# RWKV time mixing: batch 9 is transposed by the DMA crossbar instead of TensorE

## The chip, the cores and the metric

The kernel runs on one core of a Trainium2 chip. The metric is the device time of one execution in microseconds (us), the median over several runs. A core has the engines TensorE (PE, matrix products; its weight loads are listed apart as PEld), VectorE (DVE), ScalarE (ACT), GpSimd (POOL) and SyncE (SP, which here only issues transfers), and 16 DMA engines that all transfers share. Each engine works through its own instructions in order and waits on semaphores.

## The reference

16 batches of 2048 tokens with 256 channels, in float32. Each token is mixed with the one before it, by a weight for each channel; two projections, a sigmoid, a product and an output projection follow (the key projection does not reach the output).

```python
x_prev[:, 1:, :] = x[:, :-1, :]          # zeros for the first token
xv = x * time_mix_v + x_prev * (1 - time_mix_v)
xr = x * time_mix_r + x_prev * (1 - time_mix_r)
v = xv @ value_weight                    # 256 x 256 each
r = xr @ receptance_weight
out = (1 / (1 + exp(-r)) * v) @ output_weight
```

## The kernel before

**Tiling.** A batch is cut into 4 units of 512 tokens, 64 units in all, numbered through; unit 36 is the first of batch 9. The main loop runs over the units, `g`. All products run in bf16 with channels on the partitions, so x, which lies in memory with tokens in rows, has to be transposed. There are two ways:

- Batches 0 to 9: a transfer issued by POOL casts x to bf16 into an on-chip tile (`x_bf`, 4 buffers, pool `xpool`). TensorE transposes it, 8 transposes of 128 x 128 a unit (`transposes`, line 272), and ScalarE copies the result from PSUM into the transposed tile (line 289). This is done `LOOK` = 6 units ahead of use. Batches 0 and 1 have transposed tiles of their own (`xt_first0`, `xt_first1`), used by no one else afterwards; the others share tiles by groups (`GROUPS`), two buffers in turn (`xt_both`, pool `xtpool`).
- Batches 10 to 15 (from `STAGED` on): the casting transfer writes to a DRAM buffer (`x_natural`, pool `dpool`), 16 rows of zeros stand ahead of each batch (`zero_rows`), and one instruction on SP's queue reads a whole group of three batches back through the transposing crossbar into an `xt_both` tile (`by_dma`, line 254). It is issued in unit 27 for batches 10 to 12 and in unit 39 for 13 to 15 (`T_AT`).

**A unit on the engines.** The mixing is written as a scaled x plus the x of the token before, the rest of the factors being folded into the weights: two scaled tiles (for r and v) in two halves of the channels each. VectorE scales one half (line 354), POOL another (line 364, `scale_pool`, one instruction for two units), ScalarE one half of the v part from unit `FREE` on (line 638); VectorE adds (line 376). TensorE projects into `psum_r` and `psum_v` (line 384), ScalarE takes the sigmoid (line 658), VectorE multiplies into `z_sb` (line 697), TensorE makes the output product `psum_o` (line 416), ScalarE copies it to an output tile of two units (line 471), and SP stores this (line 437). `psum_r`, `psum_v` and `psum_o` have one buffer each. From unit `LATE_O` on, a unit's output product is made two units later rather than one. Output tiles take turns in 7 buffers of their own and in the 4 `x_bf` buffers once these hold no x any more (`SPARE`).

**Order.** It is the order of the code (the schedule is written by hand). Tables name the places: `LOADS` the unit whose transposes are due when a load is issued, `STAGE_AT` the units at whose end POOL issues the loads of batches 13 to 15. Three explicit dependencies tie the transfers together. A crossbar instruction waits until the last load before it has landed whole:

```python
op = nc.sync.dma_start_transpose(out=xt_both[b], in_=x_both[b].rearrange("b s d -> (b s) d"))
tc.add_manual_dep(op.ins, after.ins.name, SYNC, reason="not beside a load")
```

The loads of batches 13 to 15 wait, on POOL, until the last crossbar instruction so far (`last_t`) has landed:

```python
tc.add_manual_dep(op.ins, last_t.ins.name, SYNC, reason="not beside transposes")
```

And stores of some units (`FIRST`) wait for the first half of the last load, others (`WAITING`) are issued behind the crossbar instruction.

Of the kernel before, what the change touches and what calls it, by code (L numbers as in the profile page):

```python
# [9 lines left out]
BF16 = mybir.dt.bfloat16  # L10
# [5 lines left out]
def kernel(  # L16
# [27 lines left out]
    B, S, D = x.shape  # L44
    P = 128
    KO = D // P
    J = S // P
    UJ = 4
    TU = UJ * P
    UB = J // UJ  # L50
# [2 lines left out]
    BYUNIT = 2  # L53
    LONG = 2
    H = UJ // 2
    STAGED = 10
    BYDMA = NU - STAGED * UB
    CROSS = NU - BYDMA - LOOK
    FREE = CROSS
    LATE_O = CROSS - 2  # L60
    T_AT = {27: 10, 39: 13}
    FIRST = {19: 27, 21: 27, 27: 39}
    WAITING = {23: 27, 25: 27, 29: 39, 31: 39, 33: 39, 35: 39}
    ZEROS_AT = 12
    SINGLE = NU - 6
    STAGED_PAIRS = range(STAGED, B - 1)
    STAGE_AT = {33: 13, 34: 14, 35: 15}
    GROUPS = [(2, 3), (4, 5, 6), (7, 8, 9), (10, 11, 12), (13, 14, 15)]
    HALVED = (12, 15)
    PAD = 16  # L70
    SPARE = 9 * UB // 2
    NX, NO = 4, 7
    START_T = [1, 3, 5, 6, 7, 9, 11, 12]
    AHEAD = 6
# [7 lines left out]
        (2, 0): (5,),  # L82
        (3, 0): (6,),
        (4, 0): (7,),
        (5, 0): (8, 10),
        (6, 0): (9,),
        (7, 0): (11,),
        (7, 1): (12,),
    }

    consts = ctx.enter_context(tc.tile_pool(name="consts", bufs=1))
    xpool = ctx.enter_context(tc.tile_pool(name="xpool", bufs=NX))
    dpool = ctx.enter_context(tc.tile_pool(name="dpool", bufs=2, space=bass.MemoryType.DRAM))
    xtpool = ctx.enter_context(tc.tile_pool(name="xtpool", bufs=2))
    mixpool = ctx.enter_context(tc.tile_pool(name="mixpool", bufs=3))
    zpool = ctx.enter_context(tc.tile_pool(name="zpool", bufs=3))
# [15 lines left out]
    loads = {}  # L112
    xt_both = {}
    xt = {}
# [18 lines left out]
    def new_staged(group):  # L133

        x_both[group[0]] = dpool.tile([len(group), PAD + S, D], BF16, name="x_natural")
        for k in range(len(group)):
            x_bf[group[0] + k] = x_both[group[0]][k, PAD:].rearrange("(p j) d -> p j d", p=P)
        return [(group[0], k) for k in range(len(group))]
# [8 lines left out]
    def load(b):  # L147
        if b < STAGED:
            x_bf[b] = xpool.tile([P, J, D], BF16, name="x_bf")
        if b < BYUNIT:  # L150
            for e in range(UB):
                nc.gpsimd.dma_start(  # L152
                    out=x_bf[b][:, e * UJ : (e + 1) * UJ, :], in_=unit_rows(x, b, e)[:, 0]
                )
            return
        if b in HALVED:
            return [
                nc.gpsimd.dma_start(out=x_bf[b][:, j : j + J // 2], in_=rows(b)[:, j : j + J // 2])
                for j in (0, J // 2)
            ]  # L160
        run = 8192 if b < LONG else 16384
        return nc.gpsimd.dma_start(out=x_bf[b], in_=rows(b), max_dma_last_dim=run)  # L162
# [47 lines left out]
    def new_xt(b):  # L210
        if b >= BYUNIT:
            for group in GROUPS:
                if b != group[0]:
                    continue
                if b >= STAGED:
                    t = xtpool.tile([P, KO, len(group) * (PAD + S)], BF16, name="xt_both")
                    for k in range(len(group)):
                        xt[b + k] = t[:, :, k * (PAD + S) + PAD - 1 : (k + 1) * (PAD + S)]
                    xt_both[b] = t
                    return  # L220
                xt_both[b] = xtpool.tile([P, J + 1, KO, len(group), P], BF16, name="xt_both")
                for k in range(len(group)):
                    xt[b + k] = xt_both[b][:, :, :, k]
                    nc.gpsimd.memset(xt[b + k][:, 0, :, 0:1], 0.0)
            return
        xt[b] = consts.tile([P, UB * (UJ + 1), KO, P], BF16, name=f"xt_first{b}")
        (nc.vector if b == 0 else nc.gpsimd).memset(xt[b][:, 0, :, 0:1], 0.0)

    new_xt(0)
    tms = consts.tile([P, 2, KO], FP32)  # L230
    c_sb = consts.tile([P, 2, KO], FP32)
# [19 lines left out]
    def by_dma(b, after):  # L251

        new_xt(b)
        op = nc.sync.dma_start_transpose(
            out=xt_both[b], in_=x_both[b].rearrange("b s d -> (b s) d")
        )
        tc.add_manual_dep(op.ins, after.ins.name, SYNC, reason="not beside a load")
        return op
# [55 lines left out]
    def slots(piece, off=0):  # L314

        b, _, lo, hi = piece
        j = lo // P + (lo // TU if b < BYUNIT else 0) + off
        return slice(j, j + (hi - lo) // P)
# [6 lines left out]
    def tokens(piece, off, ko=None):  # L325

        b, _, lo, hi = piece
        if b in STAGED_PAIRS:
# [3 lines left out]
            return cols if ko is None else cols[:, ko]  # L332
        if b < STAGED:
            cols = xt[b][:, slots(piece, off)]
# [71 lines left out]
    def out_matmuls(ps, z, b, jj, n, whole=False):  # L406
# [3 lines left out]
        else:  # L410
            cols = z[:, :, jj * P : (jj + n) * P]
            order = "p k (j c) -> p k j c" if b < STAGED else "p k (c j) -> p k j c"
            slot = cols.rearrange(order, j=n)
# [35 lines left out]
    def new_o(b, h):  # L449

        n = b * UB // 2 + h - SPARE
        spare = n >= 0 and n % (NO + NX) < NX
# [109 lines left out]

    pads = [p for group in GROUPS if group[0] >= STAGED for p in new_staged(group)]
    tnext = 1

    def advance(limit):
        nonlocal tnext
        while tnext <= min(limit, NU - 1):
            b, e = divmod(tnext, UB)
            for n in LOADS.get((b, e), ()):  # L570
                loads[n] = load(n)
            if tnext < NU - BYDMA:
                transposes(tnext)
            tnext += 1
# [47 lines left out]
    for u in range(2, NU):  # L622
# [3 lines left out]
        for m, (b, _, lo, hi) in enumerate(pieces(u)):  # L626
            w = first[u][m]
            group = (b, m, lo, hi + TU if paired else hi)
# [17 lines left out]
    for g in range(NU - 1):  # L646
        ps_r = ps_r_pool.tile([P, KO, TU], FP32, name="psum_r")
        if g == 0:
            project_unmixed(ps_r, 0)
            advance(1)  # L650
            project_unmixed(ps_r, 1)
            wrap_slots(pieces(1)[0])
            scale(pieces(1)[0])
            last = add(pieces(1)[0])
        else:
            project(ps_r, g, 0)
        s_sb = zpool.tile([P, KO, TU], BF16, name="s_sb")
        nc.scalar.activation(out=s_sb, in_=ps_r, func=ACT.Sigmoid)  # L658
        advance(START_T[g] if g < len(START_T) else g + LOOK)
        if g in T_AT:  # L660
            half, whole = loads[T_AT[g] + 2]
            for pair in firsts.pop(g):
                store(nc.sync, *pair, after=half)
            last_t = by_dma(T_AT[g], whole)
            for pair in kept.pop(g, []):
                store(nc.sync, *pair)
        if LATE_O < g < NU - 2:
            output(g - 2, z_prev2)
        for p in products.get(g + 1, []):
            if g >= FREE and p[0][1] == 1:  # L670
                scale_act(p[0], (0,))
        for p in [q for q, _ in products[g]] + pooled[g]:
            last_unit_of = p[3] // TU - 1
            need = last_unit_of if p[0] < BYUNIT else min(last_unit_of + 1, UB - 1)
            assert UB * p[0] + need < tnext, (g, p, tnext)
            if g > AHEAD or p not in pooled[g]:
                wrap_slots(p)
        if g == 1:
            load(2)
            scale_act(pieces(2)[1], (1,))  # L680
        for p, kos in products[g]:
            if not (g - 1 >= FREE and p[1] == 1):
                scale(p, kos)
        for p in sums[g]:
            last = add(p)
        for p in pooled[g]:
            if p[0] >= BYUNIT:
                wrap_slots(p)
        ps_v = ps_v_pool.tile([P, KO, TU], FP32, name="psum_v")
        project(ps_v, g, 1)  # L690
        if g == 0:
            scale_act(pieces(1)[1], (0,))
            advance(2)
        z_sb = zpool.tile([P, KO, TU], BF16, name="z_sb")
        n = TU // 2 if g == NU - 2 else TU
        for c in range(0, TU, n):
            nc.vector.tensor_tensor(  # L697
                out=z_sb[:, :, c : c + n],
                in0=s_sb[:, :, c : c + n],
                in1=ps_v[:, :, c : c + n],  # L700
                op=ALU.mult,
            )
        for p in pooled[g]:
            wrap_slots(p, after=last)
            scale_pool(p, last)
        if ZEROS_AT <= g < ZEROS_AT + len(pads):
            zero_rows(*pads[g - ZEROS_AT])
        if g in STAGE_AT:
            b = STAGE_AT[g]
            loads[b] = load(b)  # L710
            for op in loads[b] if b in HALVED else [loads[b]]:
                tc.add_manual_dep(op.ins, last_t.ins.name, SYNC, reason="not beside transposes")
        for p in held[g]:
            add(p)
        if z_prev is not None and not LATE_O <= g < NU - 3:
            output(g - 1, z_prev)
        z_prev2, z_prev = z_prev, z_sb
# [31 lines left out]
```

## Time and profile before

| | us |
|---|---|
| median of 3 runs | 199.1 (198.86 to 199.21) |
| the profiled execution, first to last instruction | 197.1 |
| TensorE busy | 191.5 |
| VectorE busy | 183.1 |
| ScalarE busy | 177.1 |
| POOL busy | 86.3 |
| crossbar instructions, issue to landing (median of 2) | 17.3 |

The profile gives the profiled execution as its span; no total of its own beside that is printed. A row of instructions in time has its start, its duration, the engine, the line and operation, the tile written and those read with their shapes, how many, and in brackets the idle time of the engine before it and what ended it. "SPq" is a transfer's issue on SP's queue: its duration is that of the issue, not of the transfer. A transfer's landing is given apart, in us from its issue.

### The profile page before, as it was taken

How to read it: one execution, taken by the hardware profiler on the slowest of the kernel's cores; microseconds unless marked ns; L12 is line 12 of the kernel's file. 1: busy time of each engine (PE TensorE's matmuls, PEld its weight loads, DVE VectorE, ACT ScalarE, POOL GpSimd, SP SyncE). 2: the span in 40 equal slices, each digit the busy share in tenths (PEclk: the TensorE clock that was granted, in tenths of full speed). 3: DMA queues.
4: the chain of work that ended last, by engine and by line, in shares of the span. 5: the costliest groups of instructions: out<-in, count | busy, mean ns of one | idle time of the engine just before them, and what ended most of it. 6: DMA issues, size and time to landing. Idle time of an engine off the chain costs nothing.

```text
span 197.1 us, 3735 instructions
## 1 busy us (share of the span) xinstructions
PE 191.5 (97%) x1358; PEld 123.0 (62%) x1364; DVE 183.1 (93%) x286; ACT 177.1 (90%) x197; POOL 86.3 (44%) x117
## 2 busy tenths in 40 slices
PE   8999999999999999999999999999999999999992
PEld 3556676666666666666666666666666666666660
DVE  0999999999999999999999999999999999999962
ACT  3699899999999999999999999999999999999982
POOL 2845542443665635624334266444433444444200
PEclk9999999999999999999999999999999999999998
DMA  5999999999999999999999999999999999999985
GB/s 185 238 176 224 218 254 262 247 259 262 296 413 283 283 296 332 283 238 198 376 209 290 335 346 186 212 218 241 290 290 419 419 421 419 416 416 421 382 327 221
DMA packets 35593, 58.13 MB, mean 295 GB/s; under 512 B 26004, under 2 KB 27128, under 8 KB 30840
## 3 DMA queue, kind: packets, MB, share of 16 engines
q1 hardware_dynamic: 31792, 41.34, 60.3%
q0 software_dynamic: 3632, 16.44, 41.6%
q8 instruction: 10, 0.16, 0.3%
q10 hardware_dynamic: 152, 0.13, 0.2%
q14 instruction: 7, 0.06, 0.1%
HBM read 34.34 MB, written 39.90 MB: 377 GB/s over the span
## 4 chain that ended last, share of the span: by engine, by line
PE 90%; DMA 6%; POOL 1%; issue 0%; SPq 0%; ACT 0%
PE psum_r L384 27%; PE psum_v L384 27%; PE psum_o L416 27%; PE ps_t L272 8%; DMA x_bf<-in_x_dram 4%; DMA w_f<-n_receptance_weight_dram 2%; PE ps_t L416 1%; POOL x_bf L192 1%; SPq L174 0%; POOL wo_bf L195 0%; PE psum_v L416 0%; POOL x_bf L152 0%; PE ps_t L384 0%; PE psum_r L416 0%; ACT x_bf L446 0%
## 5 line engine op out<-in xcount | busy, mean ns | idle before, releaser
L364 POOL TENSOR_SCALAR mix<-xt_both,c_sb 128x1024 bf16<-128x1024 bf16 (+1 forms) x55 | 61.1, 1110 | 85.5 <-DVE mix L376 82.3
L697 DVE TENSOR_TENSOR z_sb<-s_sb,psum_v 128x1024 bf16<-128x1024 bf16 (+1 forms) x64 | 76.8, 1201 | 2.3 <-PE psum_v L384 1.1
L376 DVE TENSOR_TENSOR mix<-mix,xt_both 128x1024 bf16<-128x1024 bf16 x112 | 76.8, 696 | 1.4
L384 PEld LDWEIGHTS <-w_bf 128*128 128x128 bf16 x512 | 48.5, 98 | 39.2 <-DVE mix L376 0.8
L658 ACT ACTIVATE s_sb<-psum_r 128x1024 bf16<-128x1024 f32 x63 | 65.2, 1034 | 6.2 <-PE psum_r L384 6.0
L384 PE MATMUL psum_v<-mix,w_bf 128*128 128x512 bf16 (+1 forms) x252 | 64.8, 378 | 0.4 <-DVE mix L376 0.2
L384 PE MATMUL psum_r<-mix,w_bf 128*128 128x512 bf16 x250 | 64.6, 379 | 0.2
L416 PE MATMUL psum_o<-wo_bf,z_sb 128*128 128x256 bf16 x486 | 63.2, 273 | 0.0
L416 PEld LDWEIGHTS <-z_sb 128*128 128x128 bf16 x512 | 52.0, 103 | 17.9 <-DVE z_sb L510 0.7
L471 ACT COPY o_sb<-psum_o 128x1024 f32<-128x1024 f32 x50 | 51.2, 1023 | 5.0 <-PE psum_o L416 4.8
L289 ACT COPY xt_both<-ps_t 128x1024 bf16<-128x1024 bf16 x32 | 32.9, 1039 | 0.0
L272 PEld LDWEIGHTS <-x_bf 128*128 128x128 bf16 x304 | 19.8, 98 | 8.4 <-DMA x_bf<-in_x_dram 0.4
L272 PE MATMUL ps_t<-ident,x_bf 128*128 128x128 bf16 x304 | 22.7, 219 | 0.2 <-DMA x_bf<-in_x_dram 0.2
L354 DVE TENSOR_SCALAR mix<-xt_both,c_sb 128x1024 bf16<-128x1024 bf16 (+1 forms) x47 | 21.3, 463 | 0.0
L638 ACT ACTIVATE mix<-xt_both,c_sb 128x1024 bf16<-128x1024 bf16 x14 | 16.3, 1163 | 0.0
L376 DVE TENSOR_TENSOR mix<-mix,xt_first 128x1024 bf16<-128x1024 bf16 x15 | 10.5, 708 | 0.1
L471 ACT COPY x_bf<-psum_o 128x1024 f32<-128x1024 f32 x10 | 10.2, 1015 | 0.0
L354 DVE TENSOR_SCALAR mix<-xt_first,c_sb 128x512 bf16<-128x512 bf16 x22 | 6.6, 350 | 0.3 <-ACT xt_first L282 0.2
L289 ACT COPY xt_first<-ps_t 128x1024 bf16<-128x1024 bf16 x6 | 6.0, 1022 | 0.0
L557 POOL COPY xt_first<-xt_first 128x254 bf16<-128x254 bf16 x5 | 2.0, 392 | 7.2 <-DVE mix L376 7.2
L162 POOL DMA_DIRECT2D x_bf<-in_x_dram x8 | 4.7, 584 | 0.0
L364 POOL TENSOR_SCALAR mix<-xt_first,c_sb 128x512 bf16<-128x512 bf16 x6 | 4.1, 685 | 1.3 <-DVE mix L376 0.8
(68 smaller groups left out, 52.3 us busy)
## 6 DMA issues: line engine op xcount, KB each, us to landing
out_dram<-o_sb SPq DMA_DIRECT2D x25, 1024.0 KB, 12.1
x_bf<-in_x_dram POOLq DMA_DIRECT2D x8, 1024.0 KB, 15.8
x_natural<-in_x_dram POOLq DMA_DIRECT2D x4, 1024.0 KB, 11.8
out_dram<-x_bf SPq DMA_DIRECT2D x4, 1024.0 KB, 14.4
x_natural<-in_x_dram POOLq DMA_DIRECT2D x4, 512.0 KB, 12.7
out_dram<-x_bf SPq DMA_DIRECT2D x4, 512.0 KB, 4.7
x_bf<-in_x_dram POOLq DMA_DIRECT2D x6, 256.0 KB, 7.0
o_sb<-in_x_dram SPq DMA_DIRECT2D x4, 256.0 KB, 3.9
```

Source lines behind the costliest of these rows:

```text
L162: return nc.gpsimd.dma_start(out=x_bf[b], in_=rows(b), max_dma_last_dim=run)
L272: nc.tensor.transpose(out=ps[:, jj], in_=src[:, jj, ko * P : (ko + 1) * P], identity=idn)
L289: nc.scalar.copy(out=xt[b][:, j0 : j0 + UJ], in_=ps)
L354: nc.vector.tensor_scalar(out=mixed(piece, ko), in0=tokens(piece, 0, ko), scalar1=c_sb[:, m, ko : ko + 1], scalar2=None, op0=ALU.mult,)
L364: op = nc.gpsimd.tensor_scalar(out=mixed(piece, 1), in0=tokens(piece, 0, 1), scalar1=c_sb[:, m, 1:2], scalar2=1.0, op0=ALU.mult, op1=ALU.mult,
L376: return nc.vector.tensor_tensor(out=mixed(piece), in0=mixed(piece), in1=tokens(piece, 1), op=ALU.add)
L384: nc.tensor.matmul(out=ps[:, mo, :], lhsT=w_bf[:, m, ko, mo * P : (mo + 1) * P], rhs=mixed((b, m, e * TU + lo, e * TU + hi), ko), start=(k ...
L416: nc.tensor.matmul(out=ps[:, j, :], lhsT=slot[:, ko, j], rhs=wo_bf[:, ko, :], start=(ko == 0), stop=(ko == KO - 1),)
L471: nc.scalar.copy(out=o[:, j0 : j0 + UJ, :], in_=ps)
L638: nc.scalar.activation(out=mixed(piece, ko), in_=tokens(piece, 0, ko), func=ACT.Copy, scale=c_sb[:, m, ko : ko + 1],)
L658: nc.scalar.activation(out=s_sb, in_=ps_r, func=ACT.Sigmoid)
L697: nc.vector.tensor_tensor(out=z_sb[:, :, c : c + n], in0=s_sb[:, :, c : c + n], in1=ps_v[:, :, c : c + n], op=ALU.mult,)
```

## The change

Batch 9 joins the staged batches: it is cast into DRAM, gets its rows of zeros, and is transposed by a crossbar instruction of its own, issued in unit 27 just ahead of the one for batches 10 to 12. Its transposed tile is put in the memory of `xt_first0`, batch 0's tile, which moves to a pool `firstpool` of one buffer. The loads of batches 9 and 10 change places. `last_t` is, as before, the instruction for batches 10 to 12. `BYDMA` grows by 4, so `CROSS`, `FREE` and `LATE_O`, which hang on it, come down by 4 (`FREE` from 34 to 30, `LATE_O` from 32 to 28). `x_bf` buffers pass to the outputs two tiles earlier (`SPARE`).

```diff
-    STAGED = 10
+    STAGED = 9
...
-    T_AT = {27: 10, 39: 13}
+    T_AT = {27: (9, 10), 39: (13,)}
...
-    GROUPS = [(2, 3), (4, 5, 6), (7, 8, 9), (10, 11, 12), (13, 14, 15)]
+    GROUPS = [(2, 3), (4, 5, 6), (7, 8), (9,), (10, 11, 12), (13, 14, 15)]
...
-    SPARE = 9 * UB // 2
+    SPARE = STAGED * UB // 2 - 2
...
-        (5, 0): (8, 10),
-        (6, 0): (9,),
+        (5, 0): (8, 9),
+        (6, 0): (10,),
...
-    dpool = ctx.enter_context(tc.tile_pool(name="dpool", bufs=2, space=bass.MemoryType.DRAM))
+    dpool = ctx.enter_context(tc.tile_pool(name="dpool", bufs=3, space=bass.MemoryType.DRAM))
+    firstpool = ctx.enter_context(tc.tile_pool(name="firstpool", bufs=1))
...
-                    t = xtpool.tile([P, KO, len(group) * (PAD + S)], BF16, name="xt_both")
+                    pool, name = (firstpool, "xt_first0") if len(group) == 1 else (xtpool, "xt_both")
+                    t = pool.tile([P, KO, len(group) * (PAD + S)], BF16, name=name)
...
-        xt[b] = consts.tile([P, UB * (UJ + 1), KO, P], BF16, name=f"xt_first{b}")
+        xt[b] = firstpool.tile([P, UB * (UJ + 1), KO, P], BF16, name=f"xt_first{b}")
...
-            half, whole = loads[T_AT[g] + 2]
+            half, whole = loads[T_AT[g][-1] + 2]
             for pair in firsts.pop(g):
                 store(nc.sync, *pair, after=half)
-            last_t = by_dma(T_AT[g], whole)
+            for b in T_AT[g]:
+                last_t = by_dma(b, whole)
             for pair in kept.pop(g, []):
                 store(nc.sync, *pair)
```

How it stands in the queues, in two places. First SP, around the crossbar instructions; brackets name the semaphores waited for (those of transfers begin with DMAHW or DMASW). Before, ahead of it the store of a `FIRST` pair, behind it the two stores of `WAITING`, the store of the pair of units 26 and 27, and the second crossbar instruction:

```order
L437 DMA out_dram<-o_sb 128x2048 [waits DMAHW2_49,Activation_49]
L254 DMA_TRANSPOSE xt_both<-x_natural 128x2x6192 [waits DMASW5_49,DMASW1_49,DMASW6_49,DMASW0_49,DMAHW3_49,DVE_49,Pool_49]
L437 DMA out_dram<-o_sb 128x2048 [waits DMAHW4_49,Activation_49]
L437 DMA out_dram<-o_sb 128x2048 [waits DMAHW5_49,Activation_49]
L437 DMA out_dram<-o_sb 128x2048 [waits DMAHW6_49,DMASW3_49,Activation_49]
L254 DMA_TRANSPOSE xt_both<-x_natural 128x2x6192 [waits DMASW2_49,DMASW1_49,DMASW4_49,DVE_49,DMAHW7_49,Activation_49,Pool_49]
```

And in the changed kernel:

```order
L439 DMA out_dram<-o_sb 128x2048 [waits DMAHW2_49,Activation_49]
L256 DMA_TRANSPOSE xt_first_1404<-x_natural 128x2x2064 [waits DMASW5_49,DMASW1_49,DMAHW3_49,DVE_49,PE_49]
L256 DMA_TRANSPOSE xt_both<-x_natural 128x2x6192 [waits DMASW6_49,DMASW5_49,DMASW7_49,DMASW2_49,DMAHW4_49,DVE_49,Pool_49]
L439 DMA out_dram<-o_sb 128x2048 [waits DMAHW5_49,Activation_49]
L439 DMA out_dram<-o_sb 128x2048 [waits DMAHW6_49,Activation_49]
L439 DMA out_dram<-o_sb 128x2048 [waits DMAHW7_49,DMASW4_49,Activation_49]
L256 DMA_TRANSPOSE xt_both<-x_natural 128x2x6192 [waits DMASW3_49,DMASW5_49,DMASW2_49,DMASW6_49,DVE_49,DMAHW0_49,Activation_49,Pool_49]
```

The instruction for batch 9 (2064 rows) has moved in ahead of that for batches 10 to 12 (6192 rows), between the same stores.

Second POOL, from unit 33 on, where the loads of batches 13, 14 and 15 (the last in two halves) stand between its scalings. Before, the first scaling of this piece reads batch 9 in `xt_both`, and the load of batch 13 waits for the first crossbar instruction (DMAHW3):

```order
L364 TENSOR_SCALAR mix_194<-xt_both_1190,c_sb_134 128x8x128 [waits DVE_49,Activation_49]
L162 DMA x_natural_137<-in_x_dram 128x4096 [waits DMAHW3_49,DMASW1_49]
L364 TENSOR_SCALAR mix_194<-xt_both_1190,c_sb_134 128x8x128 [waits DVE_49]
L162 DMA x_natural_137<-in_x_dram 128x4096 [waits DMASW2_49]
L364 TENSOR_SCALAR mix_195<-xt_both_1190,c_sb_134 128x8x128 [waits DVE_49,PE_49]
L158 DMA x_natural_137<-in_x_dram 128x2048 [waits DMASW3_49]
L158 DMA x_natural_137<-in_x_dram 128x2048 [waits DMASW4_49]
```

In the changed kernel:

```order
L366 TENSOR_SCALAR mix_198<-xt_first0_1404,c_sb_137 128x128x2x4 [waits DMAHW3_49,DVE_49,PE_49]
L163 DMA x_natural_141<-in_x_dram 128x4096 [waits DMAHW4_49,DMASW2_49]
L366 TENSOR_SCALAR mix_198<-xt_first0_1404,c_sb_137 128x128x2x4 [waits DVE_49]
L163 DMA x_natural_141<-in_x_dram 128x4096 [waits DMASW3_49]
L366 TENSOR_SCALAR mix_199<-xt_first0_1404,c_sb_137 128x128x2x4 [waits DVE_49,PE_49]
L159 DMA x_natural_141<-in_x_dram 128x2048 [waits DMASW4_49]
L159 DMA x_natural_141<-in_x_dram 128x2048 [waits DMASW5_49]
```

The loads keep their places among the scalings; the first scaling now waits for batch 9's crossbar instruction (DMAHW3) and the load of batch 13 for the one of batches 10 to 12 behind it (DMAHW4).

## The prediction

> **What bounds the kernel now.** I read the page first: its engine shares, its slices, its DMA queues.
>
> ```profile
> span 197.1 us, 3735 instructions
> PE 191.5 (97%) x1358; PEld 123.0 (62%) x1364; DVE 183.1 (93%) x286; ACT 177.1 (90%) x197; POOL 86.3 (44%) x117
> DMA  5999999999999999999999999999999999999985
> DMA packets 35593, 58.13 MB, mean 295 GB/s; under 512 B 26004, under 2 KB 27128, under 8 KB 30840
> ```
>
> TensorE is 97% busy, so its work looks like the price of the kernel. But the DMA row is full too, from the second slice to the last but two. The profiled execution took 197.1 us from first to last instruction; its own total is not on the page, and the median of the runs, 199.1, lies 2.0 us above the span. I add all differences to 199.1.
>
> Then stretches with different traffic, each row with TensorE, weight loads, VectorE, ScalarE and POOL busy time, the granted clock (1.00 everywhere here), the share of the 16 DMA engines and their rate:
>
> ```profile
> 102.50:110.00 7.50, 7.50 (x62) 4.94 (x61) 7.18 (x11) 7.09 (x9) 2.24 (x2) 1.00 1.28 289
> 120.00:130.00 10.00, 9.95 (x61) 5.90 (x61) 9.98 (x14) 9.18 (x11) 5.18 (x6) 1.00 1.03 211
> 155.00:180.00 25.00, 24.84 (x154) 16.14 (x156) 24.94 (x34) 22.95 (x25) 11.21 (x10) 1.00 1.01 418
> ```
>
> The first is the crossbar alone, the second casting loads alone (counted by the bytes written), the third stores alone. The share is a sum over packets that can overlap, so 1.28 means full, not more than full. In each kind of traffic the engines have nothing to spare: stores run at 418 GB/s, loads at 211, crossbar transposes at 289. The kernel therefore stands against two walls, TensorE and the transfers, and VectorE (9.98 of 10, 24.94 of 25) is hard behind TensorE.
>
> Last I read the queues in order of time, at the place the change moves. SP issues the stores and the transposes, POOL its third of the mixing and the casting loads:
>
> ```profile
> 92.85 1.82 SPq L437 DMA_DIRECT2D out_dram<-o_sb  x2
> 95.38 15.20 SPq L254 DMA_TRANSPOSE xt_both<-x_natural  x1
> 110.67 0.52 SPq L437 DMA_DIRECT2D out_dram<-o_sb  x1
> ...
> xt_both<-x_natural SPq DMA_TRANSPOSE x1, 18.8
> ...
> 113.48 1.12 POOL L364 TENSOR_SCALAR mix<-xt_both,c_sb 128x1024 bf16<-128x1024 bf16 x1 [2.33 <-DVE mix L376]
> 114.71 0.56 POOL L162 DMA_DIRECT2D x_natural<-in_x_dram  x1
> 116.23 1.11 POOL L364 TENSOR_SCALAR mix<-xt_both,c_sb 128x1024 bf16<-128x1024 bf16 x1 [0.96 <-DVE mix L376]
> 117.30 0.55 POOL L162 DMA_DIRECT2D x_natural<-in_x_dram  x1
> ```
>
> The crossbar instruction for batches 10 to 12 is issued at 95.38 and lands 18.8 us later, at 114.18. The POOL instruction at 114.71 is the load of batch 13, which waits for that landing by the kernel's own rule. POOL ended its scaling at 114.60, so the landing came 0.4 us before POOL could have issued the load anyway: the wait costs nothing today, and has almost no slack.
>
> **The change, part by part.**
>
> *Taken off TensorE:* 32 transposes, 8 in each of units 30 to 33.
>
> ```profile
> 110.77 0.61 PE L272 MATMUL ps_t<-ident,x_bf 128*128 128x128 bf16 x8
> 111.21 1.04 PE L416 MATMUL psum_o<-wo_bf,z_sb 128*128 128x256 bf16 x8
> ```
>
> The next group starts 0.44 us after the transposes: 4 x 0.44 = 1.8 us less for TensorE, all on its path since it never idles there. ScalarE loses 4 evacuations and gains 2 scalings, VectorE loses 2 scalings and a small copy; so VectorE can follow at the shorter pace, as it does from unit 34 on now. All this could give is -1.8.
>
> *Added to the transfers:* the batch is read and cast as before, into DRAM instead of on-chip memory (the same bytes; its price is the loads' rate, 211 GB/s in the row above). New is its passage through the crossbar: 2064 x 256 x 2 bytes = 1.06 MB at 289 GB/s = 3.65 us. The zero rows, 8 KB, I cost at nothing: they queue behind a load.
>
> *A second instruction.* Its own start-up has no row. The nearest is the second crossbar instruction of before:
>
> ```profile
> 136.50:137.50 1.00, 1.00 (x8) 0.55 (x6) 1.00 (x2) 1.00 (x2) 0.51 (x1) 1.00 0.40 36
> xt_both<-x_natural SPq DMA_TRANSPOSE x1, 15.7
> ```
>
> Issued at 133.86, it shows a hole near its beginning: 0.60 us of the 1.00 us are empty. Its 3.17 MB at 289 GB/s take 11.0 us, so of 15.7 us issue to landing 4.7 are not flow. The bounds for the second start are thus 0 (the issue of the next runs under the packets of the first) and 4.7 (nothing overlaps). A gain below 0 is excluded: the bytes of batches 10 to 12 are the same. I take 0.5, near the hole, because both stand in one queue and SP's issue of a crossbar instruction ends before its packets do. So X, the delay of the landing for batches 10 to 12, is 3.65 + 0.5 = 4.1 us, between 3.65 and 8.4. The start does not move: both crossbar instructions still wait for the last load of batch 12, and stand behind the same two stores. The landing is then at 114.2 + 4.1 = 118.3.
>
> The Trainium skill, page "Advanced Engine Details and Errata", section "X-Bar Transpose (TRN2)", says that transposing DMAs are as fast as ordinary ones. The rows here disagree, 289 GB/s against 418, and by its rule X would be 2.5 with no other term changed, which is a rival below.
>
> *What waits for that landing.* POOL now reaches the load of batch 13 earlier, at 114.60 - 1.8 = 112.8, and stands there until 118.3. Queued behind it is its next scaling (116.23 now), then the loads of 14 and 15. The scaling feeds VectorE:
>
> ```profile
> 117.19 1.30 DVE L376 TENSOR_TENSOR mix<-mix,xt_both 128x1024 bf16<-128x1024 bf16 x2
> 118.46 1.22 DVE L697 TENSOR_TENSOR z_sb<-s_sb,psum_v 128x1024 bf16<-128x1024 bf16 x1
> 119.60 0.71 DVE L376 TENSOR_TENSOR mix<-mix,xt_both 128x1024 bf16<-128x1024 bf16 x1
> ...
> 117.33 1.03 PE L384 MATMUL psum_v<-mix,w_bf 128*128 128x512 bf16 x4
> 119.93 0.81 PE L384 MATMUL psum_v<-mix,w_bf 128*128 128x512 bf16 x3
> ```
>
> The second of the two additions (about 117.84) takes the POOL scaling that ended at 117.34, 0.5 us before. Behind it on VectorE stands the product of unit 35 (118.46 to 119.68), and that must have emptied the one psum_v bank before TensorE's next value projection, 119.93: 0.25 us of slack. Now forward: landing 118.3, load issued by 118.95, scaling to 120.06, addition to 120.7, product to 121.9, projection at 121.95 instead of 119.93. That is +2.0 against before, and the 1.8 us are already spent in it: TensorE arrives at 118.15 and waits 3.8 us. In general the shift is X + 3.65 + 114.2 - 119.93 = X - 2.1. Nothing later gives it back, since VectorE has no idle time left in the stretches from 120 to 180 above.
>
> *The transfers to the end.* Everything behind the crossbar in the queues slides by X: loads 13 to 15, the second crossbar instruction, the held stores. Is batch 13 late next? Its transposed tile lands at 133.86 + 15.7 = 149.6 now, 153.7 then. The first reader:
>
> ```profile
> 155.00 1.12 POOL L364 TENSOR_SCALAR mix<-xt_both,c_sb 128x1024 bf16<-128x1024 bf16 x1 [1.30 <-PE psum_v L384]
> ```
>
> It will be at 157.0, so 3.3 us remain, no new wait. The stores drain at 418 GB/s and arrive at the end with a backlog that is X - 2.0 = 2.1 us deeper relative to the work. Before, the transfers have holes only here:
>
> ```profile
> 186.50:187.50 1.00, 1.00 (x8) 0.55 (x6) 1.00 (x2) 1.00 (x2) 0.00 (x0) 1.00 0.62 246
> 189.50:191.00 1.50, 1.50 (x12) 1.06 (x11) 0.57 (x1) 1.27 (x4) 0.00 (x0) 1.00 0.39 156
> 192.00:194.50 2.50, 1.35 (x9) 0.54 (x8) 1.18 (x3) 1.34 (x3) 0.00 (x0) 1.00 0.79 302
> ```
>
> 0.38 + 0.91 + 0.52 = 1.8 us. So the transfers by themselves end X - 1.8 = +2.3 later. The two walls give +2.0 and +2.3; they run side by side, so the larger counts. Sum: 199.1 + 2.3 = 201.4, and I say 201.5 for the small packets at the end.
>
> *At nothing:* the other layout of batch 9's tile. POOL's scaling takes 1.12 us at 113.48 (slot layout) and 1.12 us at 155.00 (crossbar layout). The memory of batch 0's tile was read out in units 0 to 3, long before unit 27. The on-chip buffers freed for outputs change no wait that I can find: each output half still has 11 buffers in turn.
>
> **Rivals.**
>
> 1. *A dearer second start.* If the second crossbar instruction shares nothing with the first, X = 8.4: TensorE +6.3, transfers +6.6, 205.7. For it: 4.7 us of the 15.7 are not flow. Against: the first instruction's 15.20 us of issue on SP end before its landing by 3.6, so the next one starts under it. With 1.5 us of start, X = 5.2 and 202.5.
>
> 2. *Faster: the landing is not late.* The one way to gain is that POOL does not stand at the load, so that TensorE keeps its 1.8 us: 197.3. This takes a crossbar instruction whose passage for batch 9 overlaps that of 10 to 12, with X under 0.25, and the transfers' 1.8 us of holes at the end taking the rest; the price of the passage decides, and the kernel gains from X below 1.8. For it: the crossbar's packets are small, and the 289 GB/s could be the rate of one instruction rather than of the engines. Against: the share of 1.28 there, and that one queue issues both.
>
> 3. *A crossbar pass at the copy rate.* 1.06 MB at the stores' 418 GB/s is X = 2.5: TensorE +0.4, transfers +0.7, so 199.8. The Trainium skill's sentence above is this rule; the row 102.50:110.00 speaks against it. With X between 1.4 and 2.2 the time stays within 0.4 us, which is 0.2% and about what a measurement of this kernel can tell from no change.
>
> **How the numbers follow.** My own case, X from 3.65 to 5.2, 200.9 to 202.6: 0.72. Rival 1 beyond 5.2, to 205.7: 0.09. Rival 3: 0.08, a quarter of it within 0.2%. Rival 2: 0.08 faster. The remaining 0.03 is a shift within 0.2% by some cover I overlooked. Faster 0.08, same 0.05, slower 0.87. The predicted time is my case's, 201.5. The range leaves out rival 2, the no-change cases and the far end of rival 1: 199.8 (rival 3) to 203.6 (X = 6.3).
>
> **What the profile after would show.** Right: two crossbar issues in a row on SP from about 95.4, the second landing near 118; POOL idle some 5 us ahead of the load of batch 13, released by that transfer; an idle stretch of about 4 us on VectorE and then on TensorE near 118 to 122, the only one; 272 transposes on TensorE, not 304; the DMA share without holes to the end. Wrong: if the landing is before 115, the crossbar price is wrong; if it is late but TensorE has no gap, the chain POOL, VectorE, TensorE is; if the gap is there and the end is later by much more than it, the transfers are the wall alone. If the first crossbar issue comes well before 95.4, the whole sum moves with it.

## The result, and the profile after

The changed kernel takes 206.55 us (median of 4 runs, 204.94 to 206.97) against 199.16 us (198.86 to 199.56) for the kernel before beside it: ratio 1.0343, interval 1.0307 to 1.0379. Run again it took 205.25 us (204.27 to 205.43, 5 runs; ratio 1.0289, 1.0266 to 1.0311). The forecast was 201.5, from 199.8 to 203.6: the direction was right, the size was not. Ratios leave out runs that took over 1.5% longer than the fastest of their kernel, so a median over all runs can lie above what its ratio says.

From the page of the changed kernel: engine shares, granted clock and DMA row.

```profile
span 204.7 us, 3671 instructions
PE 191.4 (94%) x1324; PEld 121.7 (59%) x1332; DVE 182.1 (89%) x283; ACT 175.6 (86%) x195; POOL 87.0 (43%) x117
PEclk9999999999999999999999996999999999999997
DMA  5999999999999999999999999999999999999993
DMA packets 39785, 59.19 MB, mean 289 GB/s; under 512 B 30180, under 2 KB 31320, under 8 KB 35032
```

TensorE was not busy longer, 191.4 us against 191.5, in a span that is 7.6 us longer. The clock row has a slice at 6, which the kernel before has not. The 1.06 MB more are the pass of batch 9.

The place that the change moves: the crossbar instructions on SP's queue, then POOL's rows, from the view in order of time.

```profile
95.81 7.45 SPq L256 DMA_TRANSPOSE xt_first<-x_natural  x1
103.50 11.93 SPq L256 DMA_TRANSPOSE xt_both<-x_natural  x1
115.53 0.52 SPq L439 DMA_DIRECT2D out_dram<-o_sb  x1
...
111.83 1.12 POOL L366 TENSOR_SCALAR mix<-xt_first,c_sb 128x1024 bf16<-128x1024 bf16 x1 [1.30 <-PE psum_v L386]
119.53 0.56 POOL L163 DMA_DIRECT2D x_natural<-in_x_dram  x1 [6.58 <-DMA xt_both<-x_natural]
120.13 1.12 POOL L366 TENSOR_SCALAR mix<-xt_first,c_sb 128x1024 bf16<-128x1024 bf16 x1
```

The landings of the two crossbar instructions, from the view of transfers, in us from issue:

```profile
xt_first<-x_natural SPq DMA_TRANSPOSE x1, 10.7
...
xt_both<-x_natural SPq DMA_TRANSPOSE x1, 15.5
```

The start is where it was (95.81, before 95.38). The transfer for batches 10 to 12 lands at 103.50 + 15.5 = 119.0 (before 114.2). POOL stands for 6.58 us ahead of the load of batch 13, released by that transfer, and the scaling behind it (120.13, before 116.23) comes late. How this reaches TensorE, from the view in order of time:

```profile
121.29 0.69 DVE L378 TENSOR_TENSOR mix<-mix,xt_first 128x1024 bf16<-128x1024 bf16 x1 [5.07 <-POOL mix L366]
121.90 1.22 DVE L700 TENSOR_TENSOR z_sb<-s_sb,psum_v 128x1024 bf16<-128x1024 bf16 x1
...
117.46 1.04 PE L418 MATMUL psum_o<-wo_bf,z_sb 128*128 128x256 bf16 x8
123.17 1.79 PE L386 MATMUL psum_v<-mix,w_bf 128*128 128x512 bf16 x4 [4.67 <-DVE z_sb L700]
124.75 1.91 PE L386 MATMUL psum_r<-mix,w_bf 128*128 128x512 bf16 x4
```

And stretches of the same trace, with the columns of the prediction's (TensorE, weight loads, VectorE, ScalarE, POOL busy; clock, DMA share, GB/s): the gap, what follows it, and the end.

```profile
118.40:123.10 4.70, 0.10 (x1) 0.00 (x0) 1.81 (x3) 2.23 (x3) 3.13 (x4) 1.00 1.00 331
123.30:126.60 3.30, 3.30 (x9) 1.17 (x8) 3.04 (x5) 0.00 (x0) 2.15 (x3) 0.50 0.91 176
...
199.00:201.00 2.00, 0.00 (x0) 0.00 (x0) 0.00 (x0) 0.00 (x0) 0.00 (x0) 1.00 0.98 370
201.00:203.00 2.00, 0.00 (x0) 0.00 (x0) 0.00 (x0) 0.00 (x0) 0.00 (x0) 0.70 0.17 61
```

VectorE waits 5.07 us for POOL, TensorE 4.67 us for VectorE. Then comes what the prediction had not counted: the stretch behind the gap runs at a granted clock of 0.50, and four matmuls of 512 columns take 1.8 us instead of 1.03. TensorE's value projection of unit 36 is at 123.17 (before 119.93), +3.2; the next one at 127.45 (before 122.53), +4.9. But the last two rows say that this may not be the end's cause: TensorE finished at 198.27, and the transfers went on alone to 202.9.

So there were two readings. *The wait*: the stand on POOL sets the time, through TensorE. *The transfers*: the added pass delays all stores behind it, whatever the engines do. The experiments take them apart.

### The profile page after: what moved, and what is told of

It is laid out like the page before. It is cut to its first block, busy times and chain, and to the rows that moved or that the text cites. A ratio compares the mean times of both kernels' runs of the same rounds, so it can differ in the third digit from the quotient of the medians.

```text
span 204.7 us, 3671 instructions
## 1 busy us (share of the span) xinstructions
PE 191.4 (94%) x1324; PEld 121.7 (59%) x1332; DVE 182.1 (89%) x283; ACT 175.6 (86%) x195; POOL 87.0 (43%) x117
## 4 chain that ended last, share of the span: by engine, by line
PE 82%; DMA 10%; issue 1%; POOL 1%; DVE 1%; ACT 1%; SPq 0%; POOLq 0%
PE psum_v L386 25%; PE psum_r L386 24%; PE psum_o L418 23%; DMA xt_both<-x_natural 8%; PE ps_t L274 7%; DMA w_f<-n_receptance_weight_dram 2%; PE ps_t L418 1%; PE psum_r L400 1%; POOL mix L366 1%; DVE z_sb L700 1%; SPq L175 0%; DVE mix L378 0%; ACT mix L640 0%; PE psum_v L418 0%; POOL x_natural L163 0%
## 5 line engine op out<-in xcount | busy, mean ns | idle before, releaser
L366 POOL TENSOR_SCALAR mix<-xt_both,c_sb 128x1024 bf16<-128x1024 bf16 (+1 forms) x51 | 56.7, 1112 | 80.6 <-DVE mix L378 75.8
L660 ACT ACTIVATE s_sb<-psum_r 128x1024 bf16<-128x1024 f32 x63 | 65.1, 1034 | 13.4 <-PE psum_r L386 13.2
L378 DVE TENSOR_TENSOR mix<-mix,xt_both 128x1024 bf16<-128x1024 bf16 x104 | 71.2, 696 | 1.1
L473 ACT COPY o_sb<-psum_o 128x1024 f32<-128x1024 f32 x46 | 47.1, 1024 | 4.2 <-PE psum_o L418 4.2
L291 ACT COPY xt_both<-ps_t 128x1024 bf16<-128x1024 bf16 x28 | 28.7, 1039 | 0.0
L378 DVE TENSOR_TENSOR mix<-mix,xt_first 128x1024 bf16<-128x1024 bf16 x23 | 16.1, 709 | 5.1 <-POOL mix L366 5.1
L274 PE MATMUL ps_t<-ident,x_bf 128*128 128x128 bf16 x272 | 20.1, 219 | 0.1
L473 ACT COPY x_bf<-psum_o 128x1024 f32<-128x1024 f32 x14 | 14.2, 1015 | 0.0
L366 POOL TENSOR_SCALAR mix<-xt_first,c_sb 128x512 bf16<-128x512 bf16 (+1 forms) x10 | 8.6, 861 | 3.3 <-PE psum_v L386 1.3
L356 DVE TENSOR_SCALAR mix<-xt_first,c_sb 128x512 bf16<-128x512 bf16 (+1 forms) x24 | 7.6, 363 | 0.2
L163 POOL DMA_DIRECT2D x_natural<-in_x_dram x5 | 2.9, 570 | 6.6 <-DMA xt_both<-x_natural 6.6
```

What stands on the lines that cost most here:

```text
L274: nc.tensor.transpose(out=ps[:, jj], in_=src[:, jj, ko * P : (ko + 1) * P], identity=idn)
L291: nc.scalar.copy(out=xt[b][:, j0 : j0 + UJ], in_=ps)
L356: nc.vector.tensor_scalar(out=mixed(piece, ko), in0=tokens(piece, 0, ko), scalar1=c_sb[:, m, ko : ko + 1], scalar2=None, op0=ALU.mult,)
L366: op = nc.gpsimd.tensor_scalar(out=mixed(piece, 1), in0=tokens(piece, 0, 1), scalar1=c_sb[:, m, 1:2], scalar2=1.0, op0=ALU.mult, op1=ALU.mult,
L378: return nc.vector.tensor_tensor(out=mixed(piece), in0=mixed(piece), in1=tokens(piece, 1), op=ALU.add)
L473: nc.scalar.copy(out=o[:, j0 : j0 + UJ, :], in_=ps)
```

## The experiments

**No stand on POOL.** The loads of batches 13 to 15 are issued three units later, when the landing has happened.

```diff
-    STAGE_AT = {33: 13, 34: 14, 35: 15}
+    STAGE_AT = {36: 13, 37: 14, 38: 15}
```

> The changed kernel with the loads of batches 13, 14, 15 issued three units later (end of units 36, 37, 38), so that POOL reaches the load of batch 13 about when the crossbar instruction for batches 10 to 12 has landed (119.0). The 6.6 us stand of POOL and the 4.7 us gap of TensorE near 118 to 123 should be gone, with them the low clock behind it. If this wait is what costs the time, the kernel comes to 199.5 to 202. If the transfers are the wall by themselves, TensorE's time moves elsewhere (batch 13's crossbar instruction then lands near 156 to 157, after POOL asks for it at about 153, a new gap of some 3 us) and the time stays at 205 to 207.

205.58 us (203.99 to 208.37, 4 runs), ratio 1.0265 (1.0177 to 1.0354). Stretches of its end:

```profile
193.00:197.00 4.00, 0.00 (x0) 0.00 (x0) 0.00 (x0) 0.14 (x1) 0.00 (x0) 1.00 1.03 405
197.00:199.00 2.00, 0.00 (x0) 0.00 (x0) 0.00 (x0) 0.00 (x0) 0.00 (x0) 0.51 1.03 370
```

The gap at unit 36 and the low clock behind it are gone; TensorE ends at 192.74 (193.35 in the kernel before). The time does not come back: the ratio's interval overlaps both of the change (1.0307 to 1.0379 and 1.0266 to 1.0311), and from 193 to 199 every engine is done while the transfers are full. The wait by itself is refuted as the cause. The new gap of some 3 us that I expected at batch 13 was smaller: POOL stood for 2.17 us there (its scaling is at 154.47, released by the second crossbar instruction), and the units behind it came 0.9 us later.

**The pass alone.** The kernel before, with one more crossbar instruction whose result nobody reads; TensorE saves nothing. (Not printed here: the lines that put batch 0's tile into a pool of its own, as in the change.)

```diff
...
+            if g == 27:
+                extra = firstpool.tile([P, KO, PAD + S], BF16, name="xt_first0")
+                op = nc.sync.dma_start_transpose(
+                    out=extra, in_=x_both[10][0:1].rearrange("b s d -> (b s) d")
+                )
+                tc.add_manual_dep(op.ins, whole.ins.name, SYNC, reason="not beside a load")
```

> The kernel before, batch 9 still transposed by TensorE, with one more crossbar instruction of one batch (it reads batch 10's rows again, into the memory of batch 0's tile; nobody reads it) issued at the same place, just ahead of that for batches 10 to 12. Only the transfers are added; TensorE saves nothing. By my account TensorE's saving is swallowed whole by the wait, so this should be as slow as the change: 206 to 207, with the same gap ending at the same time (123.2), 1.8 us shorter at its front, so perhaps with less of the low clock (205). If the saving counted for itself, it would be 1.8 us slower than the change: 208.3.

204.44 us (203.79 to 206.2, 4 runs), ratio 1.0249 (1.0171 to 1.0327). That is less than the 206 to 207 that I expected, and close to the 205 given for less of the low clock. The pass alone costs about as much as the change: with its 32 transposes fewer, the changed kernel at 204.3 to 207.0 is not faster than this. The comparison is rough, since this kernel's first pass took 19.21 us against 16.66 (1.5 us of it a stall of the kind shown below). The gap is 3.26 us, from the view in order of time:

```profile
124.29 1.05 PE L385 MATMUL psum_v<-mix,w_bf 128*128 128x512 bf16 x4 [3.26 <-DVE z_sb L704]
```

And a stretch behind it, in which the clock is at 0.50 here too:

```profile
126.00:128.00 2.00, 2.00 (x9) 1.14 (x8) 2.00 (x3) 0.92 (x1) 1.11 (x1) 0.50 1.10 229
```

**Without a load.** The changed kernel without the load of batch 9; the added crossbar instruction reads batch 10's rows instead. (Not printed here: the line by which batch 9's rows of zeros are not written either.)

```diff
-        (5, 0): (8, 9),
+        (5, 0): (8,),
...
-            out=xt_both[b], in_=x_both[b].rearrange("b s d -> (b s) d")
+            out=xt_both[b],
+            in_=(x_both[10][0:1] if b == 9 else x_both[b]).rearrange("b s d -> (b s) d"),
```

> The changed kernel without the load of batch 9 and its rows of zeros (its crossbar instruction reads batch 10's rows; batch 9's output is that of batch 10). It takes 1 MB of casting load (5.0 us at 211 GB/s) out of the stream ahead of the crossbar instructions, all else equal. If the transfers alone make the change slow, the landing for batches 10 to 12 comes back to about 114 to 115, no gap, and TensorE keeps its saving: 197 to 198. If something else of the change costs time (layout, buffers, order of the output products), it stays above 199.

201.48 us (200.05 to 204.56, 10 runs), ratio 1.0054 (1.0009 to 1.0098): a miss, since I expected 197 to 198. The first pass starts 3.7 us earlier than before, at 96.47, and yet the last data of SP's stores come 3.0 us later. In place of 11.99 us the first pass with the added instruction took 17.66, 5.7 more (1.0 more than in the changed kernel, with a fetch inside it), and the second pass 1.3 more. The added pass eats a whole 1 MB load.

**The clock.** The changed kernel with 21 idle matmuls of 512 columns put ahead of unit 36's projection, where the gap is.

```diff
+        if g == 36:
+            warm_up(84)
```

> The changed kernel with 21 idle matmuls of 128x512 (about 4.55 us, constants in, results unused) ahead of the value projection of unit 36, where TensorE waits 4.7 us. The granted clock behind the gap should stay at 1.00 instead of 0.50 to 0.65 for 3.4 us, and TensorE's last matmul come 1.7 us earlier (+3.2 instead of +4.9 against before). If the end hangs on TensorE, the time falls by that, to 204.9; if it hangs on the transfers' backlog, it stays within 0.5 us of the change.

204.68 us (204.07 to 205.59, 4 runs), ratio 1.0251 (1.0181 to 1.032). The same stretch as above:

```profile
123.30:126.60 3.30, 3.26 (x20) 1.81 (x19) 3.30 (x6) 1.41 (x2) 2.23 (x4) 1.00 0.93 184
```

At 1.00 instead of 0.50, TensorE ends at 196.89, 1.4 to 1.8 us earlier than in the two traces of the changed kernel. The time is the 204.9 that I expected if the end hangs on TensorE, but it cannot be told from that of the second run of the changed kernel, in which the clock fell:

> The changed kernel once more, for its spread and another trace. Two accounts are left. Transfers alone: the stream of transfers is the wall, so the last store's data ends about 46.7 us after the last crossbar packet whatever TensorE does, and the time moves from run to run with how long the crossbar passes take. TensorE's gap: the time follows TensorE's last matmul. Expected: 204.5 to 207, last data 46.5 to 47.0 us after the last crossbar packet.

In this second trace of the changed kernel the gap and the low clock are there again and TensorE ends even later (198.73), but the last data of SP's stores come 2.2 us earlier than in the first, at 200.74.

**The stand alone.** The kernel before with the load of batch 13 issued two units early, where its wait is long.

```diff
-    STAGE_AT = {33: 13, 34: 14, 35: 15}
+    STAGE_AT = {31: 13, 34: 14, 35: 15}
```

> The kernel before with the load of batch 13 issued two units earlier (end of unit 31), so that POOL stands at it from about 108.4 until the crossbar landing at 114.2. No transfer is added. TensorE should get a gap of about 3.5 us near 115 to 118, and perhaps the half clock behind it (1.5 us more). The transfers have by then no need of TensorE, so TensorE becomes the wall: 202.6 without the low clock, 204.2 with it. If the transfers' backlog hid TensorE's delay (transfers alone are the wall of before by a wide margin), it would stay under 200.5.

Ratio 1.0101 (1.0077 to 1.0125), which rests on three runs, 201.01 to 201.67. Three others took 204.3 to 204.5, at a mean granted clock of 0.988 to 0.992 against 0.997 to 1.0 in the first three. That is near the 204.2 expected with the low clock, but no trace of such a run was kept, so the reason is not shown. In order of time:

```profile
113.67 0.56 POOL L162 DMA_DIRECT2D x_natural<-in_x_dram  x1 [4.31 <-DMA xt_both<-x_natural]
...
117.30 1.02 PE L384 MATMUL psum_v<-mix,w_bf 128*128 128x512 bf16 x4 [1.44 <-DVE z_sb L697]
```

And the stretch behind the gap:

```profile
117.30:119.00 1.70, 1.70 (x8) 0.77 (x8) 1.70 (x4) 0.65 (x1) 0.10 (x1) 1.00 1.10 241
```

POOL stood 4.31 us, but only 1.44 of it shows as a gap on TensorE; I had expected 3.5. The clock stayed at 1.00. TensorE ended at 196.13, 2.8 us later than in the kernel before; 1.0 us of this was there well ahead of the stand (the product of unit 30 on VectorE starts at 105.03, before 104.06), and 1.8 us came with it. Here the time followed TensorE: a stand on POOL does cost, where the transfers are not later still.

**The saving alone.** The kernel before without batch 9's transposes on TensorE; ScalarE copies batch 8's units in their place.

```diff
+        if b == 9:
+            nc.scalar.copy(out=xt[9][:, j0 : j0 + UJ], in_=xt[8][:, j0 : j0 + UJ])
+            return
```

> The kernel before with the 32 TensorE transposes of batch 9 left out and nothing added to the transfers (ScalarE copies batch 8's transposed units instead of the transposes' results, so batch 9's output is batch 8's). TensorE's last matmul should come 1.8 us earlier. If TensorE is the wall of before, the time falls by 1.8 to 197.3. If the transfers are, the last data still comes 46.7 us or so after the last crossbar packet, 0.4 us less than now, and the time stays at 198.6 to 199.1.

200.94 us (200.07 to 201.32, 6 runs), ratio 1.0075 (1.0051 to 1.0099): slower, with less work and no transfer added. TensorE ended at 193.31, as before; the 1.8 us did not show, so this is no clean test of what the saving is worth. VectorE and ScalarE, which lose no work here, were busy for all 3.00 us from 107 to 110 while TensorE was busy for 2.56: they held the pace. What it did show: the second pass took 14.06 us (before 12.97).

> e6_saving_alone once more (batch 9's output is batch 8's), beside e9_saving_padded on the same chip. Expected as measured: 200.1 to 201.3, a fetch of 16 KB near 140.7 inside the second crossbar pass, that pass 13.5 to 14.1 us long.

201.0 us (200.5 to 201.6, 6 runs), ratio 1.0086 (1.0066 to 1.0106), second pass 14.33 us. The row of the instruction fetches among the DMA queues between 141.0 and 141.5 (packets, MB, share):

```profile
q8 instruction: 1, 0.02, 14.9%
```

And two stretches of the pass behind it:

```profile
141.70:143.10 1.40, 1.40 (x12) 1.13 (x11) 1.40 (x3) 1.40 (x2) 1.12 (x1) 1.00 0.18 8
143.50:148.00 4.50, 4.45 (x28) 2.87 (x28) 4.49 (x7) 4.09 (x6) 2.02 (x2) 1.00 1.27 290
```

An instruction fetch of 16 KB runs at 141.2; then for 1.4 us the transfers move 8 GB/s; then 290 again. There are ten such fetches in a run. To see whose they are, and whether the stall moves with them, the same kernel got back 64 TensorE instructions (32 small idle matmuls with their weight loads, in units 1 to 8):

```diff
+        if 1 <= g <= 8:
+            for _ in range(4):
+                nc.tensor.matmul(out=ps_v[:, 0, :P], lhsT=ones, rhs=wide[:, :P], start=True, stop=True)
```

> e6_saving_alone (32 TensorE transposes left out, nothing added to the transfers, batch 9's output is batch 8's) plus 32 idle matmuls of 128x128 with their weight loads in units 1 to 8, written to the psum_v bank ahead of the value projection that overwrites it. TensorE then has as many instructions as before, so its instruction fetches (16 KB, every 256 instructions) come about when they came before. In e6 one of them fell into the second crossbar pass (140.7), and the pass stood 1.5 us. If the fetch is the cause, it moves back to about 134, the second pass takes 12.3 to 13.0 us instead of 14.1, and the time falls to 198.5 to 199.3: no gain against before, since the transfers are the wall. If the fetch has nothing to do with it, the time stays at 200.9. If TensorE were the wall, 197.3.

A stretch of its second pass:

```profile
138.00:148.00 10.00, 9.95 (x62) 6.45 (x62) 9.98 (x14) 9.18 (x11) 4.49 (x4) 1.00 1.26 286
```

The fetch moved back from 141.2 to 136.4, to the start of the pass. A hole stands there in the kernel before too, without a fetch (59 GB/s from 136.1 to 137.7; here 48 from 136.6 to 138.1); behind it the pass has no stall, and it took 12.61 us. The time fell from 201.0 to 200.28 us (199.95 to 200.67, 6 runs), ratio 1.0045 (1.0029 to 1.0062), not to 199: the idle matmuls made TensorE end 1.4 us later, and it bounds then.

**The rule itself.** The kernel before without the wait of loads 13 to 15 for the crossbar.

```diff
-                tc.add_manual_dep(op.ins, last_t.ins.name, SYNC, reason="not beside transposes")
```

> The kernel before without the rule that the loads of batches 13 to 15 wait for the crossbar landing. POOL then never stands there and the loads can fill the hole that the stream shows between the stores and the first load packets (about 0.5 us near 117). Transfers as the wall: 198.5 to 199.2, and at most the hole is gained. If loads beside a crossbar pass slow it down by more, batch 10 is late and the time rises above 200.

199.28 us (198.57 to 201.72, 12 runs), ratio 0.9987 (0.9956 to 1.0018): no difference. In the kernel before, the wait costs nothing, as the prediction had it.

## What the traces say together

From the records of single packets in each trace, and the last matmul: first and last packet of the first pass (with the added instruction where there is one) and of the second, in us. "Last data" is the end of the last packet of SP's stores. ScalarE issues one last store on its own queue; its data end 0.1 to 0.4 us later than SP's in eight of the kernels (195.76 in the kernel before) and are not counted in the table.

| kernel | first pass | second pass | TensorE's end | last data | behind TensorE | behind second pass |
|---|---|---|---|---|---|---|
| before | 100.17–112.16 | 135.29–148.26 | 193.35 | 195.40 | 2.05 | 47.14 |
| changed | 100.33–116.99 | 140.87–156.15 | 198.27 | 202.93 | 4.66 | 46.78 |
| changed, again | 100.32–116.98 | 140.63–154.12 | 198.73 | 200.74 | 2.01 | 46.62 |
| no stand | 99.82–116.84 | 140.42–153.78 | 192.74 | 200.53 | 7.79 | 46.75 |
| pass alone | 100.39–119.60 | 142.57–155.64 | 199.38 | 202.55 | 3.17 | 46.91 |
| without a load | 96.47–114.13 | 137.33–151.62 | 192.85 | 198.44 | 5.59 | 46.82 |
| clock kept | 100.29–117.06 | 140.94–154.02 | 196.89 | 200.62 | 3.73 | 46.60 |
| stand alone | 100.46–112.58 | 136.32–148.53 | 196.13 | 198.20 | 2.07 | 49.67 |
| saving alone | 100.21–112.59 | 136.85–150.91 | 193.31 | 197.74 | 4.43 | 46.83 |
| saving, again | 100.05–112.24 | 135.95–150.28 | 193.06 | 197.05 | 3.99 | 46.77 |
| saving, padded | 101.10–112.30 | 136.04–148.65 | 194.77 | 196.83 | 2.06 | 48.18 |
| no rule | 101.02–113.01 | 137.00–149.49 | 194.02 | 196.08 | 2.06 | 46.59 |

The last two columns hold the answer. The last data never come sooner than 2.0 us behind TensorE's end nor sooner than 46.6 us behind the second pass, and in every kernel one of the two is at its floor (2.01 to 2.07, or 46.6 to 46.9). These are the two walls. With ScalarE's store counted the floors are 2.4 and 46.75 to 47.25, and "pass alone" (3.5 and 47.25) then stands at the upper end of the second. In the kernel before, TensorE's floor binds, and the transfers have only 47.14 less 46.6 to 46.9, some 0.2 to 0.5 us, to spare (0.3 to 0.8 with ScalarE's store). So, by these floors, a saving on TensorE could not have gained more than that; no run tests it, since "saving alone" did not bring TensorE's end forward. Nearly every delay of the transfers is paid in full. In the changed kernel both walls moved: the transfers' to 202.9 and 200.7 in the two traces, TensorE's (its end and 2.05) to 200.3 and 200.8. Taking away the gap alone (no stand) or the clock alone (clock kept) therefore gives nothing, or too little to be told from no change.

## Why the prediction was right and wrong

*Right.* The two crossbar issues from 95.8; the saving on TensorE (the product of unit 34 starts at 114.41, before 116.06, 1.8 us earlier counted from unit 29); the crossbar's flow at 289 to 290 GB/s; the landing near 118 (119.0); the stand on POOL and its way through VectorE to TensorE, with one gap (4.67 us, forecast 3.8); 272 transposes; batch 13 not late (its first reader, at 159.93, is released by TensorE, and the pass ended at 156.15); no holes in the DMA row until its last slice. The sentence "if the gap is there and the end is later by much more than it, the transfers are the wall alone" met the first trace; the second shows that "alone" is too much. Rivals 2 and 3 fell with the landing; rival 3's X of 2.5 had also left out the second start, with the prediction's 0.5 it is 3.0 (200.3 us). Rival 1 beyond X = 5.2 fell too, since the second start took 1.0 us. The Trainium skill's rule of the crossbar at the copy rate ("Advanced Engine Details and Errata", "X-Bar Transpose (TRN2)") stays in disagreement with the first of these rows, 290 GB/s where stores run at 418:

```profile
102.00:104.50 2.50, 2.50 (x17) 1.48 (x16) 2.50 (x5) 2.48 (x3) 0.87 (x2) 1.00 1.27 290
104.50:106.30 1.80, 1.80 (x14) 1.24 (x13) 1.80 (x3) 1.80 (x3) 0.85 (x1) 1.00 0.80 94
```

*Wrong, and the main step: "the transfers to the end".* The step let the delay X be absorbed by 1.8 us of holes near the end and came to +2.3. The last data of SP's stores came 7.5 and 5.3 us later in the two traces. X itself was not far off: the landing came 4.8 us later, and with 4.8 the prediction's sum gives 199.1 + 4.8 - 1.8 = 202.1. By terms, from the table (first trace, second trace):

| term | forecast | measured |
|---|---|---|
| start of the passes | 0 | +0.2, +0.2 |
| first pass: flow of 1.06 MB and a second start | +4.1 (X) | +4.7, +4.7 |
| between the passes | 0 | +0.8, +0.5 |
| second pass | 0 | +2.3, +0.5 |
| taken up to the end | -1.8 | -0.4, -0.5 |
| sum | +2.3 | +7.5, +5.3 |

(1) The holes were read as spare from a share that is a mean over 16 engines. In the changed kernel's last row above, the share is 0.17 for 2 us: on average fewer than three of 16 engines work while the others are done. That is again 1.7 us of holes in the mean, now at the very end. A hole in the mean is not time that the last engine has; 0.4 to 0.5 us were there, not 1.8. This is the largest error common to both traces, 1.3 to 1.4 us.

(2) The first pass became 4.7 us longer, not 4.1. Of 16.66 - 11.99 = 4.67 us, 3.65 are flow and 1.0 is the second start, taken as 0.5: the row 104.50:106.30 above is that hole between the two instructions, 94 GB/s. With the start 0.2 us later, the two terms are 0.7 us more than forecast.

(3) Between the passes the loads of 13 to 15 were taken to slide by X alone. The second pass came 0.5 to 0.8 us later still. The loads' first packet stands as far behind the first pass as before (5.1 us in all three traces); the loads then took 16.9 and 16.5 us in place of 16.2, and the second pass followed them 0.1 to 0.2 us later. Why the loads took longer stays open. The slack of 0.4 us that I read at the load of batch 13 was none: POOL issues it 0.53 us behind the landing, in the changed kernel (119.00 to 119.53) as before (114.18 to 114.71), and without the rule it comes 0.2 us sooner behind the product of unit 33.

(4) The second pass was taken as of unchanged length. It was 0.5 and 2.3 us longer. In the first trace it has two stalls, one behind a fetch of 16 KB at 147.1, one at a fetch of 8 KB on another queue at 153.8:

```profile
147.20:148.70 1.50, 1.50 (x13) 1.15 (x12) 1.50 (x3) 1.50 (x2) 1.04 (x1) 1.00 1.47 62
153.90:155.00 1.10, 1.10 (x7) 0.51 (x6) 1.08 (x3) 1.07 (x2) 0.27 (x1) 1.00 1.26 107
```

In all twelve traces the second pass takes 13.5 to 15.3 us where a 16 KB fetch falls into it (five) and 12.2 to 13.4 where none does (seven, counting two with a fetch at its very start). Behind each fetch that falls into a pass clear of its start and end, the crossbar's packets nearly stop within 0.3 to 0.6 us: for 1.4 to 1.5 us behind one of 16 KB, for 0.6 to 0.9 us behind one of 8 KB. The padded kernel moved the fetch and the stall went with it, so that link is shown for the 16 KB fetch; why the crossbar stands still for it is not. The two traces of the changed kernel differ by 1.8 us with the same 16 KB fetch in both: 0.7 us of it is the stall at the 8 KB fetch, which in the second trace comes at 154.08, as the pass ends; the rest stays open.

*Wrong, the other wall.* TensorE's shift was put at +2.0. It was +3.2 at unit 36 (landing 0.7 later, and issue 0.53 behind it) and +1.7 more, +1.9 in the second trace, from the half clock at the gap, a term that was missing. With the clock kept, TensorE's end was 1.4 to 1.8 us earlier, so that price is shown. It decided nothing, because the other wall was there or farther.

That both walls come out near +5 in the second trace is also why the mechanism that I had right explains so little of the time: with POOL not standing, the loss is about the same (no stand, ratio 1.0265).

## What to carry to other kernels

Before crediting a saving on the busiest engine, measure the slack of the next wall from its own ordered work (the end of the last dependent transfer to the end of the kernel), not from dips in a mean share; here the slack was 0.2 to 0.5 us, and a pass of 3.65 us of flow cost 5.3 to 7.5. A gap of 3 us or more forecast on TensorE should carry a second term for the clock behind it, and a transposing pass a term for its own start. When instructions are added or left out, the places of the instruction fetches move with them, and a crossbar pass can change by 1.5 us for that alone.

## What was not expected of the hardware

In the traces here the crossbar stands almost still (8 and 62 GB/s in the rows above, against 290) for about 1.5 us when a 16 KB fetch of TensorE's instructions falls into its pass. The Trainium skill, "Runtime: NRT & Kernel Launch", "Instruction fetch mechanics", says that an engine's instructions are refilled in blocks of 16 KiB, 256 instructions, which agrees with ten fetches of that size here, and that crossing a block is mostly hidden. For TensorE it is (busy for all of the 1.40 us from 141.70), for the crossbar it is not.

Gaps of 3.26 and 4.67 us on TensorE were followed by a granted clock of 0.50, a gap of 1.44 us was not. In the second trace of the changed kernel, with a gap of 4.52 us, the clock was at 0.50 from within the gap on, for 6.8 us from 120.7. The Trainium skill, "TensorE: Matmul & The Clock Gate", "What's actually happening", puts the fall of the clock at an idle window of about 3.4 us; that is near the runs here, in which 3.26 us were already enough.
